# A hybrid attention layer whose engines follow a written-out list: one weight sum by an accumulating transfer, a second buffer for branch A's logarithms, other lead times

## The chip, the core and the metric

The kernel runs on one core of a Trainium2 chip. The core has a TensorE (PE, matmul, with its weight loads as PEld), a VectorE (DVE), a ScalarE (ACT), a GpSimd (POOL) and a SyncE (SP, which here only issues transfers). Each engine works off its own queue in order and waits on semaphores for the others. The metric is the device time of one execution in microseconds; the time of a kernel is the median of its runs.

## The reference, cut to what matters

One layer: a normed input, one input projection to eight parts, two kinds of attention with eight heads each, a SiLU gate, one output projection and the residual. Everything is fp32.

```python
h = rms_norm(x, norm_g)                         # (512, 2048)
qa, ka, va, ga, qb, kb, vb, gb = split(h @ w_in)   # w_in (2048, 8192), 8 parts of 1024
# branch A, stick-breaking, 8 heads of 128, strictly causal
z = qa @ ka.T * 128 ** -0.5
log_stay = where(s < t, log_sigmoid(-z), 0)
after = reverse_cumsum(log_stay) - log_stay
ya = where(s < t, exp(log_sigmoid(z) + after), 0) @ va
# branch B, 8 heads: RMS-normed q and k, learned bias by distance, softmax over the band
yb = softmax(qb_n @ kb_n.T * 128 ** -0.5 + bias) @ vb
x = x + concat(ya * silu(ga), yb * silu(gb)) @ w_out   # w_out (2048, 2048)
```

## The kernel before

**The projections.** The input projection is cut into 32 units of 256 columns (`NU`; eight head pairs `NG`, for each q, k, v and gate; even pairs belong to branch A, odd ones to B). Every product is fp32 by two fp32r parts: a high half (a cast on ScalarE) and a low half (operand minus high half, on VectorE), and matmuls of high with high, high with low, and low with high. Units are multiplied by Winograd's form of Strassen's scheme: seven products in place of eight, for which blocks of weights, blocks of activations and products are added and subtracted. Three units at the start and one at the end work in small steps; the 28 between (`MAJOR`) work with whole blocks.

**A major unit.** Its weights come as four blocks of 128 x 1024, A11, A21, A22 and A12 (`block_load`). `block_sums` forms from them on VectorE (L506) s1 = A21 + A22, s3 = A21 - A11 (in A21's place), s2 = A11 - s1 (in A11's place), and s4 = s2 + A12 (again in A11's place, after s2 has been split). `block_split` splits each of the seven operands, in the order A11, s3, s2, A22, s1, A12, s4: the high half on ScalarE (L543), the low half on VectorE (L544). There are three buffers for the split halves, so a split may begin when the operand three stages earlier has been multiplied. A stage is one operand against its activations on PE: eight matmuls of 128x512 (L803, the weights' high half against both halves of the activations) and eight of 128x256 (L805, their low half against the activations' high half). `chain` collects the products: three PSUM banks, in which several stages accumulate; after stages 0, 1 and 2 a copy of the bank to SBUF on ScalarE (L565, L568, L571), which must be done before stages 2, 3 and 4 add into that bank; later VectorE adds a bank to such a copy (L573); at the end a copy (L584) and a closing add on VectorE (L588) into the unit's result buffer, which also sets free the buffer of the copies for the next unit's L565. The result buffer must have been emptied by the attention of the head pair before.

**Attention.** `score_a` (branch A) works on a block of 128 rows: mask (L1292), absolute value (L1293), exponential (L1294), logarithm (L1295) in the buffer `L`, then relu (L1296) and a scan from the right (L1297) in the buffer `W`, a difference (L1300) and an exponential (L1302). There is one `L`, held from before the block's scores until its scan, and three `W`. `score_b` (branch B) uses a `bias` buffer, loaded once per head by `load_bias` from SP, with a memset of one corner on GpSimd (L1393). `turn` transposes the weights on PE (L1424) and splits them (L1432, L1433); `values` multiplies with v and then with the gate (L1490) and stores to DRAM; `gates` scales and applies the SiLU (L1505, L1506, with two table loads on ScalarE).

**What sets the order.** Nothing is left to the engines. While the program is being built, a small planner plays the kernel through with a clock of its own (`schedule`): every piece of work is a generator that yields conditions and operations (`Op`) with an engine, an assumed cost and a due time. Whenever an engine is free, the ready operation with the earliest due time is issued next, and that becomes the engine's instruction order. Due times are either relative to when PE will need the result (`need(k, before)`: the assumed time until product k begins, less `before`) or absolute. Without one, an operation is due `LATE` after it is announced; that holds for nearly all of attention and the SiLU. An engine that is free takes what is ready, even if its due time is far off; nothing is interrupted. On PE, attention goes ahead of projection products. Waits between engines are semaphores that follow from the data; a wrong guess of the planner costs time.

```python
self.due = due if callable(due) else (lambda d=clock[0] + LATE if due is None else due: d)
k = min(ready[e], key=lambda k: (k[0].due(), k[3]))
```

Of the kernel before, what the change touches and what calls it, by code (L numbers as in the profile page):

```python
# [72 lines left out]
def trunk_kernel(ctx: ExitStack, tc: tile.TileContext, xT, xn, wi, wqk, wo, ng, qg, kg, rel, out):  # L73
# [100 lines left out]

            self.hold = False

    LATE = 1.5

    RATE, LANDING = 290e3, 2.4

# [42 lines left out]
    def schedule(next_product):  # L223

        while True:
            while True:

                go_on = False
                for w in sorted(waiting, key=lambda w: w[0]):
                    if w in waiting and w[1]():  # L230
                        waiting.remove(w)
                        advance(w[2], w[0])
                        go_on = True
                if not go_on:
# [24 lines left out]
            while events and events[0][0] <= clock[0] + 1e-9:  # L259
                heapq.heappop(events)[2]()  # L260
# [93 lines left out]
    before_major = [n for n in olds if n < step_of[MAJOR[0], 0]]  # L354

    blocks = [1 if steps_[n][0] >= NU or len(x) > 3 and not major(steps_[n][0]) else 2 for n, x, a in program]
    takes = [(0.71 if wide(x) else 0.354 if major(steps_[n][0]) else 0.37) * b_ for (n, x, a), b_ in zip(program, blocks)]
    begins = [0.0]
    for t_ in takes:
        begins.append(begins[-1] + t_)  # L360
# [121 lines left out]
    def own(m, name):  # L482
# [4 lines left out]
        if all((m, x) in raw_ for x in RAW):  # L487
            done.add(("taken", m))

    def block_load(m, name):  # L490
        yield from own(m, name)
        k = at_step[stage(m, 5 if name == "A12" else 0 if name == "A11" else 1)]
        w = wi[chunk(MAJOR[m])]
        h, c = 2 * (name[2] == "2"), P * (name[1] == "2")

        def fn():
            for i in range(2):
                sp.dma_start(raw_[m, name][:, i * 4 * P:(i + 1) * 4 * P].rearrange("p (a b) -> p a b", b=P), w[h + i, :, :, c:c + P])

        yield Op("SP", 0.94, fn, need(k, 10), lag=P * 4096)  # L500
        done.add(("src", m, name))

    def block_sums(m):
        yield from own(m, "s1")
        r = lambda x: raw_[m, x]
        tt = lambda o, a, b, op: DV(1024, lambda: dve.tensor_tensor(out=r(o), in0=r(a), in1=r(b), op=op), need(at_step[stage(m, 1)], 6))  # L506
        k = [at_step[stage(m, p)] for p in range(NP)]
        has = lambda *x: lambda: all(("src", m, y) in done for y in x)
        yield has("A21", "A22")
        op = tt("s1", "A21", "A22", ALU.add)  # L510
        op.due = need(k[1], 5)
        yield op
        done.add(("src", m, "s1"))
        yield has("A11")
        op = tt("A21", "A21", "A11", ALU.subtract)
        op.due = need(k[1], 4)
        yield op
        done.add(("src", m, "s3"))
        yield lambda: ("w", stage(m, 0)) in done
        op = tt("A11", "A11", "s1", ALU.subtract)  # L520
        op.due = need(k[2], 4)
        yield op
        done.add(("src", m, "s2"))
        yield has("A12")
        yield lambda: ("w", stage(m, 2)) in done
        op = tt("A11", "A11", "A12", ALU.add)
        op.due = need(k[6], 4)
        yield op
        done.add(("src", m, "s4"))
        yield lambda: ("w", stage(m, 5)) in done  # L530
        unclaim(("raw", m, "A12"))

    def block_split(m, p):
        name, n, c = ORDER[p][0], stage(m, p), NP * m + p
        k = at_step[n]
        yield lambda: ("hl", c - 1) in done if c else all(("hi", x, q) in done for q in range(2) for x in having[q] if x <= before_major[-1])
        yield lambda: ("src", m, name) in done and avail(HL[c % 3])
        t = raw_[m, {"s3": "A21", "s2": "A11", "s4": "A11"}.get(name, name)]
        v = claim(("hl", c), HL[c % 3]).rearrange("p (a b) -> p a b", a=2)
        at_end.setdefault(last_of[n], []).append(("hl", c))  # L540
        mats[n] = v.rearrange("p a (b c) -> p a b c", c=P)
        done.add(("hl", c))
        yield AC(1024, lambda: act.copy(v[:, 0, :], t), need(k, 3.0))  # L543
        yield DV(1024, lambda: dve.tensor_tensor(out=v[:, 1, :], in0=t, in1=v[:, 0, :].bitcast(F32), op=ALU.subtract), need(k, 1.0))  # L544
# [7 lines left out]
    def chain(m):  # L552
# [12 lines left out]
        yield AC(512, lambda: act.copy(c[:, 0, :], b[0]), need(k[2], 1.5))  # L565
        done.add(("before", m, 2))
        yield there(1)
        yield AC(512, lambda: act.copy(c[:, 3, :], b[1]), need(k[3], 1.5))  # L568
        done.add(("before", m, 3))
        yield there(2)  # L570
        yield AC(512, lambda: act.copy(c[:, 2, :], b[0]), need(k[4], 1.5))  # L571
        done.add(("before", m, 4))
        add = lambda i, x: lambda: dve.tensor_tensor(out=c[:, i, :], in0=x, in1=c[:, i, :], op=ALU.add)  # L573
        yield there(3)
        yield DV(512, add(2, b[1]), clock[0] + 3)
        free(1)
        yield there(4)
        yield DV(512, add(3, b[0]), need(k[6], 1.5))
        done.add(("before", m, 6))
        yield there(5)  # L580
        yield DV(512, add(0, b[2]), clock[0] + 3)
# [618 lines left out]
    C = {}  # L1200
    qk, vv, wt, wT, tm, bias = {}, {}, {}, {}, {}, {}
    owner = {}
    live = dict(L=[], W=[])

    def take(who):

# [7 lines left out]

    def buffer(tag, n=1):

        ring, most = live[tag], dict(L=1, W=3)[tag]
        yield lambda: not any(ring[i] for i in range(len(ring) + n - most) if i >= 0)
        ring += [True] * n
        return [len(ring) - n + i for i in range(n)]  # L1220

    def drop(tag, i):
        live[tag][i] = False
# [36 lines left out]
    def score(g, h):  # L1260

        n = head(g, h)
        yield lambda: all(("prep", n, k) in done for k in range(2)) and (n == 0 or ("scores", n - 1) in done)
        for b in range(NT):
            i = None
            if g % 2 == 0:
                i, = yield from buffer("L")
            else:
                yield lambda: n in bias
            k, = yield from buffer("W")  # L1270
            z_ = yield from take(("score", n, b))
# [16 lines left out]
    def score_a(n, b, z_, z, L, W, w, i, k):  # L1288
# [96 lines left out]
    def load_bias(g, h):  # L1385
        n = head(g, h)

        before = n - 1 if h else n - 3
        yield lambda: ("unit", 4 * g) in done and (before < 0 or ("soft", before) in done)
        b = tmp([P, S], "bias", "bias")  # L1390
        row = rel[g // 2 * 2 + h]
        yield L_(P * 2048, lambda: sp.dma_start(b, bass.AP(tensor=row.tensor, offset=row.offset, ap=[[1, P], [1, S]])))
        yield G(0.4, lambda: pool.memset(b[0:CHUNK, 0:CHUNK], NEG_BIG))  # L1393
        bias[n] = b

    def score_b(n, b, z_, z, p_, w, k):
        st = tmp([P, 2], "st", "st", bufs=4)
# [208 lines left out]
```

## Time and profile before

| | |
|---|---|
| runs | 918.74, 919.42, 920.57 us; median 919.42 |
| profiled execution | 919.27 us, span 917.5 us, granted clock 0.998 |
| busy | PE 903.3, weight loads 802.3, VectorE 824.1, ScalarE 635.5, GpSimd 17.8 us |
| weight sums on VectorE (L506) | 112 of 128x1024, 136.3 us, 1217 ns each |
| splits (L543 on ScalarE, L544 on VectorE) | 196 each, 206.3 and 237.8 us |
| weight loads from `wi` on SP | 254 of 256 KB, 3.5 us median to landing |
| accumulating transfers on GpSimd (L1090) | 12 of 256 KB, from HBM into SBUF, in the last 130 us |

The page gives each engine's busy share of the span, the span in 40 slices, the transfer queues, the chain of work that ended last, the costliest groups of instructions with the idle time of their engine in front of them and what ended it, and the transfers. A busy PE is not PE at its peak, since matmuls are pipelined and their ends modelled. The groups' names are source lines; "L803 <-ACT arena L565 2.8" is 2.8 us in which PE stood ahead of a matmul of line 803 until ScalarE's instruction of line 565 had ended.

### The profile page before, as it was taken

What the parts mean: (1) busy time and instruction counts of PE and PEld (TensorE: products, weight loads), DVE (VectorE), ACT (ScalarE), POOL (GpSimd) and SP (SyncE); (2) the same over time, 40 slices, a digit from 0 to 9 for tenths busy, and PEclk for the clock granted to TensorE, in tenths of its full rate; (3) what the DMA queues carried; (4) which work ended last, traced back from release to release, by engine and by line L of the source; (5) the groups of instructions that cost most, each with busy time, mean ns of one, the idle gap of its engine ahead of it and who ended that gap; (6) DMA issues with size and microseconds to landing.
All of it is one profiled execution on the core that took longest, in us unless ns stands there. A gap on an engine that the chain in (4) does not pass through costs nothing.

```text
span 917.5 us, 15033 instructions
## 1 busy us (share of the span) xinstructions
PE 903.3 (98%) x5504; PEld 802.3 (87%) x5504; DVE 824.1 (90%) x1307; ACT 635.5 (69%) x1202; POOL 17.8 (2%) x35
## 2 busy tenths in 40 slices
PE   9999999999999999999999999999999999999997
PEld 6898888878888888888888888888888988899997
DVE  8989899979998998998989989999998998978785
ACT  8775777697687668875877688658778885634342
POOL 0000000000000000000000000000000000101011
PEclk9999999999999999999999999999999999999999
DMA  9663343323332433333333333333332536656371
GB/s 321 210 204 93 83 124 93 104 80 91 109 101 73 135 104 92 102 105 104 93 92 115 107 92 101 117 106 96 94 102 76 150 115 217 170 188 171 129 184 47
DMA packets 149914, 112.14 MB, mean 122 GB/s; under 512 B 7248, under 2 KB 126544, under 8 KB 149840
## 3 DMA queue, kind: packets, MB, share of 16 engines
q1 hardware_dynamic: 147696, 107.51, 38.2%
q0 software_dynamic: 1728, 3.15, 2.1%
q8 instruction: 43, 0.70, 0.3%
q10 hardware_dynamic: 416, 0.52, 0.2%
q14 instruction: 31, 0.25, 0.1%
HBM read 102.77 MB, written 8.39 MB: 121 GB/s over the span
## 4 chain that ended last, share of the span: by engine, by line
PE 83%; DVE 7%; ACT 6%; issue 2%; DMA 1%; SPq 0%; DVEq 0%; ACTq 0%
PE banks L803 36%; PE banks L805 18%; PE banks L732 16%; PE banks L730 8%; PE banks L1424 2%; PE banks L793 1%; DMA arena<-in_wi 1%; DVE parts L449 1%; DVE parts L544 1%; PE banks L1326 1%; ACT parts L543 1%; PE banks L1447 1%; DVE arena L506 1%; PE banks L794 1%; DVE xt L675 1%
## 5 line engine op out<-in xcount | busy, mean ns | idle before, releaser
L803 PE MATMUL banks<-x,parts 128*128 128x512 f32 x1568 | 503.1, 402 | 5.5 <-ACT arena L565 2.8
L805 PEld LDWEIGHTS banks<-x,parts 128*128 128x128 f32 x1568 | 294.3, 188 | 72.9 <-DVE parts L544 3.8
L805 PE MATMUL banks<-x,parts 128*128 128x256 f32 x1568 | 311.2, 280 | 0.5 <-DVE parts L544 0.4
L543 ACT CAST parts<-arena 128x1024 fp32r<-128x1024 f32 x196 | 206.3, 1057 | 100.6 <-PE banks L803 59.4
L544 DVE TENSOR_TENSOR parts<-arena,parts 128x1024 fp32r<-128x1024 f32 x196 | 237.8, 1219 | 17.4 <-ACT parts L543 17.0
L803 PEld LDWEIGHTS banks<-x,parts 128*128 128x128 f32 x1568 | 241.4, 190 | 7.9 <-ACT arena L565 3.4
L506 DVE TENSOR_TENSOR arena<-arena 128x1024 f32<-128x1024 f32 x112 | 136.3, 1217 | 3.9 <-DMA arena<-in_wi 3.8
L732 PE MATMUL banks<-parts,x 128*128 128x256 f32 (+1 forms) x672 | 134.6, 298 | 0.0
L445 ACT CAST parts<-arena 128x1024 fp32r<-128x1024 f32 (+3 forms) x84 | 77.2, 926 | 76.6 <-PE banks L732 39.5
L732 PEld LDWEIGHTS banks<-parts,x 128*128 128x128 f32 x672 | 107.4, 191 | 4.1 <-DVE parts L449 0.4
L449 DVE TENSOR_TENSOR parts<-arena,parts 128x1024 fp32r<-128x1024 f32 (+3 forms) x84 | 89.3, 1070 | 20.9 <-ACT parts L445 20.5
L730 PE MATMUL banks<-parts,x 128*128 128x256 f32 (+1 forms) x336 | 100.2, 298 | 0.0
L732 PE MATMUL banks<-x,parts 128*128 128x256 f32 (+1 forms) x320 | 75.4, 327 | 0.5 <-DVE parts L449 0.3
L730 PEld LDWEIGHTS banks<-parts,x 128*128 128x128 f32 x336 | 63.9, 190 | 3.3
L573 DVE TENSOR_TENSOR arena<-banks,arena 128x512 f32<-128x512 f32 x84 | 57.3, 683 | 9.0 <-PE banks L805 8.9
L732 PEld LDWEIGHTS banks<-x,parts 128*128 128x128 f32 x320 | 53.8, 190 | 7.0 <-DVE parts L449 2.0
L730 PE MATMUL banks<-x,parts 128*128 128x256 f32 (+1 forms) x160 | 52.9, 331 | 0.0
L1432 ACT CAST wth<-banks 128x128 fp32r<-128x128 f32 (+1 forms) x64 | 27.5, 430 | 10.9 <-PE banks L1424 10.8
L1433 DVE TENSOR_TENSOR wtl<-banks,wth 128x128 fp32r<-128x128 f32 (+1 forms) x64 | 31.0, 485 | 4.1 <-ACT wth L1432 4.1
L588 DVE TENSOR_TENSOR c<-arena 128x1024 f32<-128x1024 f32 x28 | 34.1, 1218 | 0.0
L730 PEld LDWEIGHTS banks<-x,parts 128*128 128x128 f32 x160 | 30.5, 191 | 3.3 <-ACT parts L445 0.5
L1424 PE MATMUL banks<-ident,W 128*128 128x128 f32 x160 | 28.4, 276 | 1.1 <-DVE wtl L1433 0.7
(206 smaller groups left out, 1085.3 us busy)
## 6 DMA issues: line engine op xcount, KB each, us to landing
arena<-in_wi SPq DMA_DIRECT2D x254, 256.0 KB, 3.5
arena<-in_wo SPq DMA_DIRECT2D x64, 256.0 KB, 3.9
xs<-in_xn SPq DMA_DIRECT2D x16, 256.0 KB, 4.3
mixd<-c SPq DMA_DIRECT2D x16, 256.0 KB, 2.3
out<-co SPq DMA_DIRECT2D x16, 256.0 KB, 5.1
x<-mixd SPq DMA_DIRECT2D x12, 256.0 KB, 3.9
co<-in_xn POOLq DMA_DIRECT2D x12, 256.0 KB, 6.4
x<-in_xT SPq DMA_DIRECT2D x8, 256.0 KB, 5.4
```

Source lines behind the costliest of these rows:

```text
L445: act.copy(whl[n, part][:, 0, c], t)
L449: yield DV(c.stop - c.start, lambda: dve.tensor_tensor(out=l[:, c], in0=t, in1=h[:, c].bitcast(F32), op=ALU.subtract), need(k, 0.5))
L506: tt = lambda o, a, b, op: DV(1024, lambda: dve.tensor_tensor(out=r(o), in0=r(a), in1=r(b), op=op), need(at_step[stage(m, 1)], 6))
L543: yield AC(1024, lambda: act.copy(v[:, 0, :], t), need(k, 3.0))
L544: yield DV(1024, lambda: dve.tensor_tensor(out=v[:, 1, :], in0=t, in1=v[:, 0, :].bitcast(F32), op=ALU.subtract), need(k, 1.0))
L573: add = lambda i, x: lambda: dve.tensor_tensor(out=c[:, i, :], in0=x, in1=c[:, i, :], op=ALU.add)
L588: yield DV(1024, lambda: dve.tensor_tensor(out=t_, in0=c[:, :, :H], in1=c[:, :, H:], op=ALU.add), clock[0] + 1.5)
L730: pe.matmul(o, lh, rh, start=start, stop=False, **kw)
L732: pe.matmul(o, x, y, start=False, stop=stop and (x is ll) != early, **kw)
L803: pe.matmul(both, mats[n][:, 0, j, :], X[j][:, :, i, :], start=p in (0, 1, 5) and j == 0, stop=False, skip_group_check=True)
L805: pe.matmul(o[:, :H], mats[n][:, 1, j, :], X[j][:, 0, i, :], start=False, stop=j == NJ - 1, skip_group_check=True)
L1424: pe.transpose(t[:, j * P:(j + 1) * P], src[:, j * P:(j + 1) * P], ident)
```

## The change

Four things are changed.

- s4 is no longer a VectorE instruction. An accumulating transfer, issued by GpSimd, adds A12 to the buffer that holds s2, both in SBUF (28 transfers, 512 KB each). The planner assumes 1.1 us for its issue and 7 us until it has landed, and its due time is 14 us ahead of stage 6.
- Branch A's logarithms may use the `bias` buffer when `L` is taken, except for the last block of a pair's second head (`either`). The bias load of the first head of a pair of branch B waits for that last block to begin, and the load is kept in a ring of one (`live["bias"]`).
- Lead times: `LATE` is 4.5 in place of 1.5; the sums s1 and s3 are due 4.5 and 3.5 us ahead in place of 5 and 4 (s2 stays at 4), a split's high half 2.5 in place of 3.0, its low half 1.5 in place of 1.0, the three bank copies 1.0 in place of 1.5, the add ahead of stage 6 2.0 in place of 1.5.
- The planner's assumed time of a major product is 0.351 in place of 0.354 us in `takes`; a membership test in its loop is dropped. Two expressions of `block_load` become functions (`piece`, `source`).

```diff
-    LATE = 1.5
+    LATE = 4.5
+
+    AHEAD = 4.5, 3.5, 4, 2.5, 1.5, 1.0, 2.0
...
-                    if w in waiting and w[1]():
+                    if w[1]():
...
-    takes = [(0.71 if wide(x) else 0.354 if major(steps_[n][0]) else 0.37) * b_ for (n, x, a), b_ in zip(program, blocks)]
+    takes = [(0.71 if wide(x) else 0.351 if major(steps_[n][0]) else 0.37) * b_ for (n, x, a), b_ in zip(program, blocks)]
...
-        op.due = need(k[1], 5)
+        op.due = need(k[1], AHEAD[0])
...
-        op.due = need(k[1], 4)
+        op.due = need(k[1], AHEAD[1])
...
-        op.due = need(k[2], 4)
+        op.due = need(k[2], AHEAD[2])
         yield op
         done.add(("src", m, "s2"))
         yield has("A12")
         yield lambda: ("w", stage(m, 2)) in done
-        op = tt("A11", "A11", "A12", ALU.add)
-        op.due = need(k[6], 4)
-        yield op
+        yield G(1.1, lambda: pool.dma_start(r("A11"), r("A12"), accum_op=ALU.add), need(k[6], 14))
+        there = clock[0] + 7.0
+        later(there, lambda: None)
+        yield lambda: clock[0] >= there - 1e-9
         done.add(("src", m, "s4"))
...
-        yield AC(1024, lambda: act.copy(v[:, 0, :], t), need(k, 3.0))
-        yield DV(1024, lambda: dve.tensor_tensor(out=v[:, 1, :], in0=t, in1=v[:, 0, :].bitcast(F32), op=ALU.subtract), need(k, 1.0))
+        yield AC(1024, lambda: act.copy(v[:, 0, :], t), need(k, AHEAD[3]))
+        yield DV(1024, lambda: dve.tensor_tensor(out=v[:, 1, :], in0=t, in1=v[:, 0, :].bitcast(F32), op=ALU.subtract), need(k, AHEAD[4]))
...
-        yield AC(512, lambda: act.copy(c[:, 0, :], b[0]), need(k[2], 1.5))
+        yield AC(512, lambda: act.copy(c[:, 0, :], b[0]), need(k[2], AHEAD[5]))
...
-        yield DV(512, add(3, b[0]), need(k[6], 1.5))
+        yield DV(512, add(3, b[0]), need(k[6], AHEAD[6]))
...
-    live = dict(L=[], W=[])
+    live = dict(L=[], W=[], bias=[])
...
+    def either(other):
+
+        yield lambda: not any(live["L"]) or other and not any(live["bias"])
+        tag = "bias" if any(live["L"]) else "L"
+        live[tag].append(True)
+        return tag, len(live[tag]) - 1
...
             if g % 2 == 0:
-                i, = yield from buffer("L")
+                last = h and b == NT - 1
+                if last:
+                    done.add(("last", n))
+                i = yield from either(not last)
...
-            L = tmp([P, S], "L", "L")[:, :w] if g % 2 == 0 else None
+            L = tmp([P, S], i[0], "L")[:, :w] if g % 2 == 0 else None
...
-        drop("L", i)
+        drop(*i)
...
-        before = n - 1 if h else n - 3
-        yield lambda: ("unit", 4 * g) in done and (before < 0 or ("soft", before) in done)
+        yield lambda: ("unit", 4 * g) in done and (("soft" if h else "last", n - 1) in done)
+        k, = yield from buffer("bias")
         b = tmp([P, S], "bias", "bias")
...
         bias[n] = b
+        yield lambda: ("soft", n) in done
+        drop("bias", k)
```

More of the change, by code (lines that the diff above doesn't have):

```diff
@@ L488, in own, with piece, source @@
             done.add(("taken", m))
+    def piece(m, name, i):
+        return raw_[m, name][:, i * 4 * P:(i + 1) * 4 * P].rearrange("p (a b) -> p a b", b=P)
+    def source(m, name, i):
+        h, c = 2 * (name[2] == "2"), P * (name[1] == "2")
+        return wi[chunk(MAJOR[m])][h + i, :, :, c:c + P]
     def block_load(m, name):
@@ L492, in block_load @@
         k = at_step[stage(m, 5 if name == "A12" else 0 if name == "A11" else 1)]
-        w = wi[chunk(MAJOR[m])]
-        h, c = 2 * (name[2] == "2"), P * (name[1] == "2")
         def fn():
             for i in range(2):
-                sp.dma_start(raw_[m, name][:, i * 4 * P:(i + 1) * 4 * P].rearrange("p (a b) -> p a b", b=P), w[h + i, :, :, c:c + P])
+                sp.dma_start(piece(m, name, i), source(m, name, i))
         yield Op("SP", 0.94, fn, need(k, 10), lag=P * 4096)
@@ L564, in chain @@
         c = claim(("cmb", m), CMB).rearrange("p (a b) -> p a b", a=4)
-        yield AC(512, lambda: act.copy(c[:, 0, :], b[0]), need(k[2], 1.5))
+        yield AC(512, lambda: act.copy(c[:, 0, :], b[0]), need(k[2], AHEAD[5]))
         done.add(("before", m, 2))
         yield there(1)
-        yield AC(512, lambda: act.copy(c[:, 3, :], b[1]), need(k[3], 1.5))
+        yield AC(512, lambda: act.copy(c[:, 3, :], b[1]), need(k[3], AHEAD[5]))
         done.add(("before", m, 3))
         yield there(2)
-        yield AC(512, lambda: act.copy(c[:, 2, :], b[0]), need(k[4], 1.5))
+        yield AC(512, lambda: act.copy(c[:, 2, :], b[0]), need(k[4], AHEAD[5]))
         done.add(("before", m, 4))
@@ L1215, in buffer @@
     def buffer(tag, n=1):
-        ring, most = live[tag], dict(L=1, W=3)[tag]
+        ring, most = live[tag], dict(L=1, W=3, bias=1)[tag]
         yield lambda: not any(ring[i] for i in range(len(ring) + n - most) if i >= 0)
```

## Prediction

> **What bounds the kernel now.** First the page's engine totals, then PE and the other engines in five stretches cut where the work changes: start, first heads, steady units, hand-over to the output projection, output projection. (Columns: stretch, length, busy us and count per engine, granted clock, DMA share, GB/s.)
>
> ```profile
> PE 903.3 (98%) x5504; PEld 802.3 (87%) x5504; DVE 824.1 (90%) x1307; ACT 635.5 (69%) x1202; POOL 17.8 (2%) x35
> ...
> 0.00:70.00 70.00, 68.08 (x356) 57.70 (x357) 62.07 (x107) 53.45 (x100) 2.21 (x10) 1.00 0.75 241
> 70.00:207.00 137.00, 131.46 (x766) 114.97 (x765) 124.27 (x196) 102.24 (x203) 0.29 (x2) 0.99 0.33 97
> 207.00:690.00 483.00, 482.52 (x2857) 424.66 (x2856) 446.55 (x662) 355.61 (x692) 0.73 (x5) 1.00 0.35 101
> 690.00:760.00 70.00, 68.68 (x431) 60.45 (x430) 63.03 (x137) 59.45 (x129) 0.94 (x2) 1.00 0.38 123
> 760.00:917.50 157.50, 152.59 (x1100) 144.53 (x1099) 128.15 (x209) 64.74 (x80) 13.61 (x16) 1.00 0.53 155
> ```
>
> PE is the bound, and its 5504 matmuls are not touched. It is idle 14.17 us in all: 1.92, 5.54, 0.48, 1.32 and 4.91 us by stretch. The first is the start and the last the tail behind the last matmul, where this change has nothing; so there are 7.3 us of plain idle time to win, three quarters of it in the 137 us from 70 to 207. The 483 us after that are already full. Next, whom PE waits for, from the groups by line:
>
> ```profile
> L803 PE MATMUL banks<-x,parts 128*128 128x512 f32 x1568 | 503.1, 402 | 5.5 <-ACT arena L565 2.8 <-ACT arena L568 2.1 <-ACT arena L571 0.6
> L805 PEld LDWEIGHTS banks<-x,parts 128*128 128x128 f32 x1568 | 294.3, 188 | 72.9 <-DVE parts L544 3.8
> L543 ACT CAST parts<-arena 128x1024 fp32r<-128x1024 f32 x196 | 206.3, 1057 | 100.6 <-PE banks L803 59.4 <-issue 13.7 <-DVE arena L506 13.6
> L544 DVE TENSOR_TENSOR parts<-arena,parts 128x1024 fp32r<-128x1024 f32 x196 | 237.8, 1219 | 17.4 <-ACT parts L543 17.0
> L506 DVE TENSOR_TENSOR arena<-arena 128x1024 f32<-128x1024 f32 x112 | 136.3, 1217 | 3.9 <-DMA arena<-in_wi 3.8
> ```
>
> So the stops are not for DVE's weight sums. They are for ScalarE's copies of a finished stage's bank (L565, L568, L571: 5.5 us), and in small pieces for the low half of a split (L544: 3.8 us, seen by the weight loads). The largest of them, in order of time (start, length, instruction, idle before it):
>
> ```profile
> 192.99 1.28 ACT L1505 ACT_TABLE_LOAD   x1
> 194.29 1.06 ACT L1505 ACTIVATE c<-c 128x1024 f32<-128x1024 f32 x1
> 195.37 1.28 ACT L1506 ACT_TABLE_LOAD   x1
> 196.66 0.60 ACT L1407 ACTIVATE W<-W,st,yn 128x256 f32<-128x256 f32 x1
> ...
> 198.41 0.73 ACT L1407 ACTIVATE W<-W,st,yn 128x384 f32<-128x384 f32 x1
> 199.02 0.22 ACT L1407 ACTIVATION_READ_ACCUMULATOR W<-W,st,yn 128x1 f32 x1
> 199.11 0.60 ACT L568 COPY arena<-banks 128x512 f32<-128x512 f32 x1
> 199.76 0.73 PE L803 MATMUL banks<-x,parts 128*128 128x512 f32 x2 [2.06 <-ACT arena L568]
> ```
>
> ScalarE stood 3.7 us in the SiLU and its two table loads, and then ran 2.45 us of attention (196.66 to 199.11) before the copy that PE was waiting for.
>
> **The change part by part.**
>
> *Lead times.* Work without a due time of its own (all of attention, and the SiLU) becomes due 4.5 us after it is announced, not 1.5. The splits' high half moves from 3.0 to 2.5 us ahead of its stage, the low half from 1.0 to 1.5, the bank copies from 1.5 to 1.0. Copies and high halves keep their order among themselves; both pass attention more easily, by 2.5 us of due time. I go through PE's stops one by one.
>
> (a) Stop at 199.76. The copy would follow the table load at 196.65 and be done by 197.25, before PE ran dry at 197.7: 2.06 us. The clock falls behind it as well:
>
> ```profile
> 200.00:204.00 4.00, 4.00 (x16) 3.44 (x16) 2.75 (x5) 4.00 (x8) 0.00 (x0) 0.57 0.25 66
> ```
>
> A granted clock of 0.57 over 4 us is 4 x 0.43 = 1.7 us. Together 3.8 us. (The Trainium skill, "TensorE: Matmul & The Clock Gate", section "HAM oscillation — how this bites in real kernels", asks for idle gaps of over about 3.4 us before the clock is gated. By it this stop of 2.06 us would not be the cause, the term would be 2.1 and the time 1.7 us higher. The trace has the drop right behind the stop, and I go by the trace.)
>
> (b) and (c) Two smaller stops:
>
> ```profile
> 118.55 1.29 DVE L1245 TENSOR_TENSOR qk<-c,qk 128x512 fp32r<-128x512 f32 x2
> 119.75 1.23 DVE L544 TENSOR_TENSOR parts<-arena,parts 128x1024 fp32r<-128x1024 f32 x1
> 120.89 1.23 DVE L588 TENSOR_TENSOR c<-arena 128x1024 f32<-128x1024 f32 x1
> ...
> 121.84 1.05 ACT L543 CAST parts<-arena 128x1024 fp32r<-128x1024 f32 x1
> 122.77 0.60 ACT L565 COPY arena<-banks 128x512 f32<-128x512 f32 x1
> 123.43 0.73 PE L803 MATMUL banks<-x,parts 128*128 128x512 f32 x2 [1.43 <-ACT arena L565]
> ...
> 105.40 0.58 ACT L1293 ACTIVATE L<-banks,rstds 128x384 f32<-128x384 f32 x1
> 105.88 0.36 ACT L1432 CAST wth<-banks 128x256 fp32r<-128x256 f32 x1
> 106.13 0.60 ACT L571 COPY arena<-banks 128x512 f32<-128x512 f32 x1
> 106.78 0.72 PE L803 MATMUL banks<-x,parts 128*128 128x512 f32 x2 [0.59 <-ACT arena L571]
> ```
>
> At 123.43 the copy L565 waited for the buffer that the closing add L588 frees. That add keeps its due time and passes the two L1245 (1.29 us); but a split stands between it and the copy as before, so I take 0.9 of the 1.43 us. At 106.78 L1293 and L1432 stood ahead (0.94 us): all 0.6 us go. The remaining L565 share, 2.8 - 1.43 = 1.4 us, is a stop at 78.9 behind the closing adds of the last plain unit, whose dues stay: 0.
>
> (d) The low halves: 3.8 us of waits at most. They are due 0.5 us earlier and DVE is lighter (below); I take half, 1.9.
>
> (e) A new order has stops of its own. Over the 27 units from 70 to 690 PE idles (5.54 + 0.48) / 27 = 0.22 us per unit; I charge a third of that to each of 28: 2.1 us against, bounds 0 and 28 x 0.22 = 6.2.
>
> *The fourth sum.* 28 of the 112 sums (L506) leave DVE: 28 x 1.217 = 34.1 us of its 824. Since PE waits for DVE for 3.8 us in all, they are worth no more than what (d) has. In exchange GpSimd issues 28 accumulating transfers of 512 KB. The trace has no such transfer inside SBUF; the nearest is the residual's, 256 KB from HBM:
>
> ```profile
> L1090 POOL DMA_DIRECT2D co<-in_xn x12: 862/920/1235, 789.0 to 877.3; - x12
> DMA to landing us min/median/max: 3.5/6.4/8.6
> ```
>
> With twice the bytes the landing lies between 3.5 us and 2 x 8.6 = 17.2 us; I take 8, the median and a quarter, near the list's own 1.1 + 7.0. There is a window for it. In one of the shorter units, the low half of stage 2's split (after which A11 may be overwritten), the old sum, the split of the sum, its low half and stage 6 itself stand at
>
> ```profile
> 493.29 1.20 DVE L544 TENSOR_TENSOR parts<-arena,parts 128x1024 fp32r<-128x1024 f32 x1
> ...
> 498.06 1.22 DVE L506 TENSOR_TENSOR arena<-arena 128x1024 f32<-128x1024 f32 x1
> ...
> 501.59 1.06 ACT L543 CAST parts<-arena 128x1024 fp32r<-128x1024 f32 x1
> ...
> 505.26 1.22 DVE L544 TENSOR_TENSOR parts<-arena,parts 128x1024 fp32r<-128x1024 f32 x1
> 507.19 0.72 PE L803 MATMUL banks<-x,parts 128*128 128x512 f32 x2
> ```
>
> The sum must be there 1.06 + 1.22 us before 507.19, at 504.9: 10.4 us after 494.49. Eight fit, so the term is 0; the cover is stages 2 to 5 on PE. If it is late, the split L543 stands waiting on ScalarE with bank copies and attention queued behind it, and PE waits for those. On POOL's queue only the eight bias memsets stand in its way, each waiting for its bias load. The transfers add 28 x 0.5 = 15 MB to stretches with a DMA share of 0.33 to 0.35; weight loads are issued up to 10 us ahead: 0.
>
> *Logarithms in two buffers.* The next block's absolute value no longer waits for the scan before it. The bias buffer lends itself, so the bias load comes later, after the last block of the heads before, and waits on SP with weight loads behind it (10 us ahead). Branch A's end is not what PE waits for, with one exception:
>
> ```profile
> 168.03 0.69 DVE L1490 TENSOR_TENSOR c<-banks,c 128x512 f32<-128x512 f32 x1
> ...
> 169.90 1.22 DVE L588 TENSOR_TENSOR c<-arena 128x1024 f32<-128x1024 f32 x1
> ...
> 171.16 0.59 ACT L565 COPY arena<-banks 128x512 f32<-128x512 f32 x1
> ```
>
> The first pair's product with its gate (L1490) frees the buffer that L588 writes, and the next unit's copy follows at once. Two buffers bring this forward, later dues push it back; I take 0, bounds -1.4 us and the rival below. The planner's stage price of 0.351 for 0.354 and the dropped membership test move due times by under 0.1 us in 10: 0.
>
> **Sum.** 3.8 + 0.9 + 0.6 + 1.9 - 2.1 = 5.1 us off the profiled execution's 919.27 us (span 917.5 us and 1.8 around it): 914.2. The median of the runs is 919.42, 0.15 above that execution: 914.3 us.
>
> **The rivals.**
>
> *The stops stay.* Where a split became ready just before a copy (123.43), priority does not matter, because the engine was free; the list's clock may differ from the chip's at the SiLU too. Against it: at 199 and 106 only default work stood ahead. Then (c) and half of (d) remain, 1.5 us, with 0.5 us of new stops: 918.4, no change.
>
> *Attention becomes the bound (slower).* From L1490 at 168.03 to the copy's end at 171.75 there is no slack. Behind the pair's last scan come five steps on ScalarE and VectorE (L1300, the exponential L1302, the transposed weights' high half L1432 and low half L1433, L1490 itself). If each now loses to one split (1.06 or 1.22, mean 1.14 us), L1490 comes 5.7 us later; L588, the copy and PE stop as long, and a stop over 2.06 us brings the clock's 1.7 us. From L1490 at 168.0 on, each us costs one. For it: ScalarE is 75% and DVE 91% busy there. Against it: two buffers and 1.2 us less DVE work per unit. 914.3 + 7.4 = 921.7 us.
>
> *The transfer is late (slower).* It decides from 10.4 us. At 12 us a unit like the one shown loses 1.6 us; were a fifth of the 28 so short, 9 us: 923.3. For it: 8.6 us already at half the bytes. Against it: those rows come several at once and from HBM, these singly and inside SBUF.
>
> *The change does not do what it says.* If due times hardly decide who is next, the list is nearly the same with 28 sums gone: that is the first rival's time.
>
> **How the numbers follow.** Forecast 0.62, stops stay 0.16, attention 0.13, late transfer 0.06, the rest 0.03. The forecast's own range is 909 to 917.5: down to (a) to (d) with the stop at 123 and (d) whole and no new one (919.4 - 3.8 - 1.4 - 0.6 - 3.8 = 909.8, less 0.5 for the steady stretch's idle), up to new stops at 5.3. The bounds let the time fall by 5.5 + 1.7 + 0.5 + 1.3 + 3.8 = 12.8 at the very most, 906.6. For 8 in 10 I give 907.5 to 922, which takes in the unchanged case and the attention rival. A measurement of this kernel can tell about 0.2%, 1.8 us, from no change. Faster by more than that: 0.62 and a quarter of the first rival, 0.66; within it 0.14; slower 0.20.
>
> **What would show it.** L506 x84 and 28 transfers on POOL landing in under 10 us; PE's idle time from 70 to 207 at 2 us or less and the clock there at 1.00; L803's wait on L568 and L571 gone, that on L565 near 1.4; L805's wait on L544 halved; 207 to 690 under 2.5 us idle. Wrong if L803 waits for a split behind a late sum, if L588 follows a late L1490 near 168 us, or if the steady stretch shows new stops over 6 us.

## The result, and the profile after

The changed kernel takes 913.00 us (median of four runs, 912.89 to 913.28) against 919.17 us for the kernel before beside it: ratio 0.9931, 95% interval 0.9914 to 0.9948, 6.2 us faster. The forecast was 914.3. The profiled execution has a span of 910.8 us, 6.7 less than before.

The page's engine totals, then PE and the others in the same stretches (columns as in the prediction):

```profile
PE 899.3 (99%) x5504; PEld 801.8 (88%) x5504; DVE 793.7 (87%) x1279; ACT 634.2 (70%) x1199; POOL 42.2 (5%) x63
...
0.00:70.00 70.00, 67.97 (x356) 57.61 (x357) 62.01 (x107) 53.41 (x100) 2.37 (x10) 1.00 0.75 241
70.00:207.00 137.00, 133.46 (x786) 116.75 (x786) 120.80 (x186) 100.23 (x196) 5.51 (x7) 1.00 0.46 118
207.00:690.00 483.00, 482.02 (x2861) 425.64 (x2860) 424.57 (x653) 360.20 (x711) 19.08 (x27) 1.00 0.50 125
690.00:760.00 70.00, 70.00 (x438) 62.85 (x437) 63.48 (x137) 58.80 (x117) 1.77 (x3) 1.00 0.49 155
760.00:910.80 150.80, 145.88 (x1071) 138.96 (x1069) 122.79 (x201) 61.52 (x75) 13.45 (x16) 1.00 0.52 151
```

PE's idle time by stretch is now 2.03, 3.54, 0.98, 0 and 4.92 us, 2.7 less in all: 2.0 less with the first heads, 1.3 less at the hand-over, 0.5 more in the steady units. The other 4 us are in PE's busy time for the same 5504 matmuls (903.3 to 899.3): 1.7 of them were the spell at half clock behind the stop at 199.8, which is gone (the first heads' granted clock is 1.00, not 0.99); for the other 2.3 no row names a cause. That they are waits which a matmul's modelled end hides is a guess. From the groups by line:

```profile
L811 PE MATMUL banks<-x,parts 128*128 128x512 f32 x1568 | 502.3, 402 | 3.4 <-ACT arena L573 2.4
L813 PEld LDWEIGHTS banks<-x,parts 128*128 128x128 f32 x1568 | 294.3, 188 | 71.5 <-DVE parts L552 2.0
L513 DVE TENSOR_TENSOR arena<-arena 128x1024 f32<-128x1024 f32 x84 | 102.2, 1216 | 6.1 <-DMA arena<-in_wi 5.9
L533 POOL DMA_DIRECT2D arena<-arena x28 | 24.4, 873 | 563.3 <-DMA arena<-in_wi 219.3
```

Lines have moved: matmuls L803 and L805 are L811 and L813, splits L543 and L544 are L551 and L552, the copies after stages 0, 1 and 2 (first, second and third copy below) L565, L568, L571 are L573, L576, L579, the closing add L588 is L596, the gate product L1490 is L1510. PE's waits for copies fell from 5.5 to 3.4 us, for low halves from 3.8 to 2.0.

ScalarE around the SiLU that made the largest stop before (start, length, instruction):

```profile
193.46 0.58 ACT L576 COPY arena<-banks 128x512 f32<-128x512 f32 x1
194.06 1.28 ACT L1525 ACT_TABLE_LOAD   x1
195.35 1.06 ACT L1525 ACTIVATE c<-c 128x1024 f32<-128x1024 f32 x1
196.43 1.28 ACT L1526 ACT_TABLE_LOAD   x1
197.72 0.59 ACT L579 COPY arena<-banks 128x512 f32<-128x512 f32 x1
198.21 0.49 ACT L1427 ACTIVATE W<-W,st,yn 128x128 f32<-128x128 f32 x1
```

The second copy now stands ahead of the SiLU, the third directly behind its table load, and attention after that. Before, 2.45 us of attention stood in between.

The transfer, from the view of its line:

```profile
L533 POOL DMA_DIRECT2D arena<-arena x28: 859/868/1021, 76.9 to 693.0; - x28
DMA to landing us min/median/max: 4.6/5.6/6.4
```

By these views most of the signs that the prediction named are there: 84 sums, 28 transfers landing in under 10 us, the clock at 1.00 from 70 to 207, the waits for low halves about halved, 0.98 us of idle time in the steady units. Three are not: PE is idle for 3.54 us from 70 to 207, not 2 or less; it still waits 1.0 us for second and third copies (0.8 for L576, 0.2 for L579); and it waits 2.4 us for first copies, not 1.4. The experiments show that the forecast's terms were not the whole of it.

### The profile page after: what moved, and what is told of

It is laid out like the page before. It is cut to its first block, busy times and chain, and to the rows that moved or that the text cites. A ratio compares the mean times of both kernels' runs of the same rounds, so it can differ in the third digit from the quotient of the medians.

```text
span 910.8 us, 15157 instructions
## 1 busy us (share of the span) xinstructions
PE 899.3 (99%) x5504; PEld 801.8 (88%) x5504; DVE 793.7 (87%) x1279; ACT 634.2 (70%) x1199; POOL 42.2 (5%) x63
## 3 DMA queue, kind: packets, MB, share of 16 engines
q0 software_dynamic: 5760, 17.83, 12.4%
## 4 chain that ended last, share of the span: by engine, by line
PE 82%; DVE 9%; ACT 4%; DMA 3%; issue 2%; SPq 0%; DVEq 0%; ACTq 0%
PE banks L811 34%; PE banks L813 17%; PE banks L740 17%; PE banks L738 8%; DVE parts L552 2%; DMA arena<-in_wi 2%; PE banks L1444 2%; PE banks L801 1%; DVE arena L513 1%; PE banks L1344 1%; DVE parts L451 1%; ACT parts L551 1%; PE banks L802 1%; PE banks L1467 1%; DVE xt L683 1%
## 5 line engine op out<-in xcount | busy, mean ns | idle before, releaser
L811 PE MATMUL banks<-x,parts 128*128 128x512 f32 x1568 | 502.3, 402 | 3.4 <-ACT arena L573 2.4
L813 PEld LDWEIGHTS banks<-x,parts 128*128 128x128 f32 x1568 | 294.3, 188 | 71.5 <-DVE parts L552 2.0
L813 PE MATMUL banks<-x,parts 128*128 128x256 f32 x1568 | 310.0, 279 | 1.1 <-DVE parts L552 1.1
L551 ACT CAST parts<-arena 128x1024 fp32r<-128x1024 f32 x196 | 205.7, 1053 | 114.1 <-PE banks L811 49.9
L552 DVE TENSOR_TENSOR parts<-arena,parts 128x1024 fp32r<-128x1024 f32 x196 | 237.9, 1217 | 41.4 <-ACT parts L551 40.6
L811 PEld LDWEIGHTS banks<-x,parts 128*128 128x128 f32 x1568 | 240.6, 189 | 5.7 <-ACT arena L573 3.1
L513 DVE TENSOR_TENSOR arena<-arena 128x1024 f32<-128x1024 f32 x84 | 102.2, 1216 | 6.1 <-DMA arena<-in_wi 5.9
L581 DVE TENSOR_TENSOR arena<-banks,arena 128x512 f32<-128x512 f32 x84 | 57.1, 680 | 7.0 <-PE banks L813 5.5
L533 POOL DMA_DIRECT2D arena<-arena x28 | 24.4, 873 | 563.3 <-DMA arena<-in_wi 219.3
L596 DVE TENSOR_TENSOR c<-arena 128x1024 f32<-128x1024 f32 x28 | 34.0, 1214 | 0.0
```

What stands on the lines that cost most here:

```text
L551: yield AC(1024, lambda: act.copy(v[:, 0, :], t), need(k, AHEAD[3]))
L596: yield DV(1024, lambda: dve.tensor_tensor(out=t_, in0=c[:, :, :H], in1=c[:, :, H:], op=ALU.add), clock[0] + 1.5)
L811: pe.matmul(both, mats[n][:, 0, j, :], X[j][:, :, i, :], start=p in (0, 1, 5) and j == 0, stop=False, skip_group_check=True)
L813: pe.matmul(o[:, :H], mats[n][:, 1, j, :], X[j][:, 0, i, :], start=False, stop=j == NJ - 1, skip_group_check=True)
```

## The experiments

Theory 1 was the prediction's: the later due time carries the gain, the sum off VectorE is worth the low halves' waits at most, the second log buffer nothing. Theory 2: the 34 us less on VectorE carry it. Theory 3: every new order has stops of its own, and no part carries anything.

**Each part undone.**

```diff
# no_late: the changed kernel with
-    LATE = 4.5
+    LATE = 1.5
# no_sum: the changed kernel with
-        yield G(1.1, lambda: pool.dma_start(r("A11"), r("A12"), accum_op=ALU.add), need(k[6], 14))
-        there = clock[0] + 7.0
...
+        op = tt("A11", "A11", "A12", ALU.add)
+        op.due = need(k[6], 4)
+        yield op
# no_ahead: the changed kernel with
-    AHEAD = 4.5, 3.5, 4, 2.5, 1.5, 1.0, 2.0
+    AHEAD = 5, 4, 4, 3.0, 1.0, 1.5, 1.5
# no_logs: the changed kernel with buffer("L") for either(...), and load_bias as before
-                i = yield from either(not last)
+                i, = yield from buffer("L")
```

> The changed kernel with the default due time back at 1.5 us, all else as changed. Theory 1 (the default due time carries the gain, because attention no longer stands ahead of bank copies on ScalarE): 917 to 919 us, bank-copy waits of PE back at 4 us or more, among them one of about 2 us during a SiLU with a clock drop behind it. Theory 2 (the 34 us taken off VectorE carry it): 913 to 914.5 us. Theory 3 (every new order has its own stops by chance, no part carries the gain): anywhere from 912 to 918.

> The changed kernel with the fourth sum back on VectorE (due 4 us ahead of stage 6, as before). Theory 1: 913 to 915 us, at most the 1.8 us by which the waits on low halves fell come back. Theory 2: 917 to 919 us, PE waiting for low halves again for 3.8 us. Theory 3: 912 to 918.

> The changed kernel with the lead times of sums, splits and bank copies as before (5, 4, 4, 3.0, 1.0, 1.5, 1.5), default due time 4.5. Theory 1: 913 to 914.5 us, since copies and high halves keep their order among themselves and only the low halves lose 0.5 us. Theory 2: 913 to 914.5 too. Theory 3: 912 to 918.

> The changed kernel with one buffer for branch A's logarithms and the bias load's old condition. Theory 1: 913 to 914 us in the steady stretch; but the later due times then fall on a chain with one buffer, so if the first pair's gate product (at 168 us in the kernel before) comes later, PE loses as much there, up to 4 us: 913 to 917. Theory 2: 913. Theory 3: 912 to 918.

Measured against 919.27 us for the kernel before beside them: no_late 931.51 us (ratio 1.0131, 1.0108 to 1.0154), no_sum 918.56 (0.9993, 0.9984 to 1.0003), no_ahead 919.75 (1.0006, 0.9997 to 1.0016), no_logs 937.87 (1.0203, 1.0188 to 1.0218). Without any one of these four the gain is gone, and without either of two of them (the due time, the buffers) the kernel is far slower than before. All three theories fall: 18.5 us for the due time is more than it could have gained, the buffer priced at nothing is worth 24.9, and no range for luck reached that far.

**Each part alone.**

```diff
# late_only: the kernel before with
-    LATE = 1.5
+    LATE = 4.5
# sum_only: the kernel before with the accumulating transfer in place of
-        op = tt("A11", "A11", "A12", ALU.add)
# logs_only: the kernel before with either(...) and the new load_bias in place of
-                i, = yield from buffer("L")
# takes_only: the kernel before with
-0.354 if major
+0.351 if major
```

> The kernel before with the default due time at 4.5 us in place of 1.5, nothing else. Theory 1: 915 to 916 us, the stops at 106 and 199 us and the clock drop gone, no or smaller stop at 123. Theory 2: 919. Theory 3: 914 to 921. The rival of the prediction (attention becomes the bound): 920 to 922, with L588 behind a late L1490 near 168 us.

> The kernel before with the fourth sum as an accumulating transfer, nothing else. Theory 1: 917.5 to 919 us, the stops on bank copies stay and only waits on low halves fall by 1 to 2 us. Theory 2: 914 to 915. Theory 3: 914 to 921.

> The kernel before with branch A's logarithms in two buffers and the later bias load, nothing else. Theory 1 and 2: 918.5 to 919.5 us. Theory 3: 914 to 921.

> The kernel before with the planner's price of a major product at 0.351 in place of 0.354, nothing else: a change of due times by under 0.1 us in 10, made to see how much a new order alone moves the time. Theory 1 and 2: 918.5 to 919.5 us. Theory 3: it moves by 1 us or more to either side, with stops in other places.

Measured against 919.44 us beside them: late_only 938.94 us (1.0210, 1.0194 to 1.0225), sum_only 939.17 (1.0209, 1.0194 to 1.0225), logs_only 927.88 (1.0080, 1.0060 to 1.0099), takes_only 921.17 (1.0011, 1.0002 to 1.0021). None of the four helps alone, and all ranges of theories 1 and 2 were missed; theory 3's held for takes_only alone. The last run says what a new order by itself does: ScalarE's list is the same for its first half and then differs, and the time moves by 1.7 us. So 2 us could be luck. One such run sets no limit to what luck can do; that 8 to 25 us are more than luck rests on the pairs and the steps of the due time below.

Where the time goes differs with the part. With the later due time and one log buffer, much of it is the chain at which the prediction saw its slower rival. late_only, the first pair's gate product, the closing add, the first copy, and PE:

```profile
180.46 0.69 DVE L1490 TENSOR_TENSOR c<-banks,c 128x512 f32<-128x512 f32 x1 [3.23 <-PE banks L732]
...
181.33 1.22 DVE L588 TENSOR_TENSOR c<-arena 128x1024 f32<-128x1024 f32 x1
...
182.58 0.59 ACT L565 COPY arena<-banks 128x512 f32<-128x512 f32 x1 [0.68 <-DVE c L588]
...
183.22 1.22 PE L803 MATMUL banks<-x,parts 128*128 128x512 f32 x2 [2.80 <-ACT arena L565]
```

The gate product comes 12.4 us later than before (168.03), after VectorE has stood idle for 3.23 us, the copy stands behind the closing add, and PE stops; it had already stopped 2.8 us at 174 for the pair's transposed weights. The pair's last scan shows where the delay comes from. In the kernel before, late_only, no_logs and the changed kernel:

```profile
156.63 1.22 DVE L1297 TENSOR_TENSOR_SCAN W<-L,W 128x512 f32<-128x512 f32 x1
...
165.88 1.22 DVE L1297 TENSOR_TENSOR_SCAN W<-L,W 128x512 f32<-128x512 f32 x1
...
169.16 1.22 DVE L1305 TENSOR_TENSOR_SCAN W<-L,W 128x512 f32<-128x512 f32 x1
...
152.29 1.23 DVE L1315 TENSOR_TENSOR_SCAN W<-L,W 128x512 f32<-128x512 f32 x1 [0.36 <-ACT W L1314]
```

With one buffer, 9.3 (late_only) and 12.5 us (no_logs) of delay are there before the last scan starts, in the blocks that take the buffer one after the other. With two, in the changed kernel, the scan starts 4.3 us earlier than before and the steps behind it take 4.3 us longer, so the gate product stays at 168.

The longest stop of late_only is another one, 4.14 us, behind a closing add that stood behind two L1245 (1.28 us) on a busy VectorE, the stop (b) of the prediction grown:

```profile
125.21 1.21 DVE L588 TENSOR_TENSOR c<-arena 128x1024 f32<-128x1024 f32 x1
...
127.09 1.22 PE L803 MATMUL banks<-x,parts 128*128 128x512 f32 x2 [4.14 <-ACT arena L565]
```

The clock adds to it: granted 0.95 from 70 to 207, against 0.99 before, is 6.9 us lost in that stretch against 1.7. Attention's last pair is late as well: the hand-over has 2.9, 1.5 and 1.2 us of stops for it. no_logs shows both again (gate product at 177.8 us, 2.9, 1.5 and 1.2 us at the hand-over).

With the old due time and new buffers or a lighter VectorE, ScalarE fills with attention in front of the second and third copies. no_late, ScalarE and PE at the last SiLU but one:

```profile
713.89 1.28 ACT L1525 ACT_TABLE_LOAD   x1
715.18 1.06 ACT L1525 ACTIVATE c<-c 128x1024 f32<-128x1024 f32 x1
716.26 1.28 ACT L1526 ACT_TABLE_LOAD   x1
717.55 0.21 ACT L1142 ACTIVATE rq<-nwt 128x4 f32<-128x4 f32 x1
...
718.94 0.71 ACT L1391 ACTIVATE qk<-c,qgs 128x512 fp32r<-128x512 f32 x1
719.55 0.57 ACT L576 COPY arena<-banks 128x512 f32<-128x512 f32 x1
...
720.17 0.73 PE L811 MATMUL banks<-x,parts 128*128 128x512 f32 x2 [3.09 <-ACT arena L576]
```

That is the stop of term (a) again, 3.1 us long: SiLU, then 2 us of attention, then the copy. sum_only has it twice at 4.3 us, at 392 and 580 us, in the same way. no_late also has 4.2 us of PE's waits for VectorE's add of a bank to a copy (L581), of which the kernel before and the changed one have none.

So a second theory, theory A below (theory B is chance): default due time and log buffers pull on two ends. Early dues put attention in front of the copies, and a second buffer makes more attention ready to stand there. Late dues make attention late, and the second buffer pays that back. They are right only together.

**The two together, and neither.**

```diff
# late_logs: the kernel before with
-    LATE = 1.5
+    LATE = 4.5
-                i, = yield from buffer("L")
+                i = yield from either(not last)
# no_late_no_logs: the changed kernel with the reverse
```

> The kernel before with both the default due time of 4.5 us and the two buffers for branch A's logarithms, sums on VectorE and lead times as before. Theory A (the two belong together: the later due time alone makes attention late, the second buffer alone sets more attention ahead of the bank copies): 917 to 924 us, far under the 938.9 and 927.9 of each alone; the first pair's last gate product back near 168 us, PE waiting under 1.5 us for the copies after stages 1 and 2. Theory B (a new order moves the time by chance): no relation to the two, anything from 915 to 940. If the gains of single parts simply added: 919 + 20 + 8 = 947.

> The changed kernel with default due time 1.5 us and one buffer for the logarithms: left are the accumulating transfer and the lead times. Theory A: no late attention (first pair's last gate product at 168 to 172 us, hand-over as before), but attention ahead of the copies: PE waits 3 to 12 us for the copies after stages 1 and 2, 922 to 936 us. Theory B: anything from 915 to 940. If undoing added: 913 + 18 + 25 = 956.

Measured against 919.11 us beside them: late_logs 919.98 us (1.0008, 0.9999 to 1.0018), no_late_no_logs 942.62 (1.0255, 1.0240 to 1.0270). The medians in two squares:

| | due 1.5, one buffer | due 4.5, one buffer | due 1.5, two buffers | due 4.5, two buffers |
|---|---|---|---|---|
| sum on VectorE, old lead times | 919.3 (before) | 938.9 | 927.9 | 920.0 |
| accumulating transfer, new lead times and stage price | 942.6 | 937.9 | 931.5 | 913.0 (changed) |

Added up, the single losses would have given late_logs 947 us; together they cancel to 920. Theory A holds there. In the second row no_late_no_logs came out 6.6 us above its range, with 13.1 us of waits for the second copy, and its hand-over was not as before (4.4 us idle, granted clock 0.95): the transfer, the new lead times and the stage price, without the pair, belong with the early-due failure. They pay only on top of the pair, 920.0 to 913.0. late_logs loses most of that at the hand-over, 2.84 us of idle time and 3.5 by the clock:

```profile
690.00:760.00 70.00, 67.16 (x410) 59.20 (x410) 57.38 (x127) 56.49 (x122) 0.88 (x2) 0.95 0.39 129
```

One half of theory A is seen in the first row only. There the second buffer alone raises the waits for the second and third copies (2.7 to 7.0 us, next table) and the time. In the second row it lowers both (13.1 to 9.2 us, 942.6 to 931.5), and the later due time alone gains too (937.9). The other half holds in both rows: with late dues the second buffer brings the gate product forward, from 180.5 to 167.2 and from 177.8 to 168.0.

**The due time moved either way.**

```diff
# late_3 and late_6: the changed kernel with
-    LATE = 4.5
+    LATE = 3.0     # late_3; 6.0 in late_6
```

> The changed kernel with a default due time of 3.0 us in place of 4.5. Theory A: the first pair's last gate product earlier than 168 us (155 to 166), PE's waits for the copies after stages 1 and 2 between the 1.0 us at 4.5 and the 9.2 us at 1.5: 914 to 924 us. Theory B: no trend, 912 to 930.

> The changed kernel with a default due time of 6.0 us in place of 4.5. Theory A: the copies after stages 1 and 2 cost PE 1 us at most, but the first pair's last gate product comes at 169 to 175 us and L588 with its stop behind it, and the hand-over to the output projection has stops again: 914 to 924 us. Theory B: no trend, 912 to 930.

Measured against the same 919.11 us: late_3 916.19 us (0.9973, 0.9963 to 0.9983), late_6 935.61 (1.0180, 1.0165 to 1.0195). Side by side, PE's waits for the second and third copies (from the waits of PE) and the start of the first pair's last gate product (from the timeline):

| kernel | default due | log buffers | second and third copy, us | gate product, us | time, us |
|---|---|---|---|---|---|
| before | 1.5 | 1 | 2.7 | 168.0 | 919.3 |
| sum_only | 1.5 | 1 | 12.3 | 171.6 | 939.2 |
| takes_only | 1.5 | 1 | 2.7 | 168.5 | 921.2 |
| logs_only | 1.5 | 2 | 7.0 | 146.7 | 927.9 |
| no_late | 1.5 | 2 | 9.2 | 151.4 | 931.5 |
| no_late_no_logs | 1.5 | 1 | 13.1 | 168.9 | 942.6 |
| late_3 | 3.0 | 2 | 3.2 | 157.0 | 916.2 |
| changed | 4.5 | 2 | 1.0 | 168.0 | 913.0 |
| late_logs | 4.5 | 2 | 1.0 | 167.2 | 920.0 |
| no_ahead | 4.5 | 2 | 1.2 | 165.7 | 919.8 |
| no_sum | 4.5 | 2 | none | 173.9 | 918.6 |
| late_only | 4.5 | 1 | none | 180.5 | 938.9 |
| no_logs | 4.5 | 1 | none | 177.8 | 937.9 |
| late_6 | 6.0 | 2 | 0.7 | 174.3 | 935.6 |

Along the due time both columns go the way theory A says: every kernel due at 1.5 waits 2.7 to 13.1 us for these copies, every one due at 4.5 or later at most 1.2; and the gate product moves later with the due time (151, 157, 168, 174 for two buffers and the transfer). The columns do not give the time: no_sum and late_6 are nearly alike in both and 17 us apart. late_6 has the late gate product and the stops at the hand-over that were expected, but is 12 us over its range. Its waits show, beside the chain at the gate product, 3.1 us for VectorE's adds of a bank (L581; 3.4 in no_late_no_logs), which theory A does not explain, and stops for splits of the mixed activations at the end (late_logs and no_ahead have fewer):

```profile
PE banks L740 <- DVE xbbias L726: 1.2, 1, 1.2
PE banks L740 <- DVE xbwth L726: 1.0, 1, 1.0
PE banks L738 <- ACT xbbias L725: 1.0, 1, 1.0
PE banks L740 <- DVE x L726: 0.9, 1, 0.9
```

In the program these splits wait until the last pair's attention has released the buffers in which they are made, so attention that is late at the end holds them up.

**What the transfer is worth where the pair is in place.** no_sum against the changed kernel: the steady units are as good (483 us with 0.06 us idle), the hand-over too (0.01 idle); all of the 5.6 us are lost with the first heads:

```profile
70.00:207.00 137.00, 128.85 (x751) 112.43 (x750) 122.12 (x196) 98.08 (x197) 0.29 (x2) 0.99 0.32 93
207.00:690.00 483.00, 482.94 (x2866) 426.48 (x2865) 446.07 (x664) 360.06 (x700) 0.72 (x5) 1.00 0.35 101
690.00:760.00 70.00, 69.99 (x447) 63.26 (x446) 65.44 (x137) 60.00 (x127) 0.88 (x2) 1.00 0.43 139
```

```profile
173.93 0.69 DVE L1509 TENSOR_TENSOR c<-banks,c 128x512 f32<-128x512 f32 x1 [0.68 <-PE banks L739]
...
174.60 1.22 DVE L595 TENSOR_TENSOR c<-arena 128x1024 f32<-128x1024 f32 x1
...
176.50 0.88 PE L810 MATMUL banks<-x,parts 128*128 128x512 f32 x2 [2.61 <-ACT arena L572]
```

The gate product at 173.9, 6 us later than with the transfer, then the closing add, the first copy and PE: 2.6 us, after 2.3 us at 169 for the same pair's weights, and a spell at half clock behind them (0.99 over the stretch). That is the chain of late_only in small. VectorE is 89% busy there; the sums taken off it bring the first pair's attention back to 168. In the kernel before, PE's direct waits for VectorE, where the prediction looked, do not show this.

The new lead times alone on the kernel before were not run, and the stage price was not undone in the changed kernel. no_ahead loses 6.8 us against the changed kernel, from the steady units on, with more waits for low halves (changed: 2.0 us); which of the seven numbers does it is open.

```profile
L813 PEld LDWEIGHTS banks<-x,parts 128*128 128x128 f32 x1568 | 294.3, 188 | 73.0 <-DVE parts L552 4.3
```

## Why the prediction was right, and where it was not

The time, the sign and the range held: 5.1 us forecast, 6.2 measured. Term by term:

- (a) The stop at 199.8 and its half clock are gone (3.8 forecast, 3.8 found), though not quite as described: the second copy, for which PE stopped, now passes the SiLU as well, and it is the third that directly follows the table load. With the stop the half clock went; here the row was a better guide than the 3.4 us of the Trainium skill, "TensorE: Matmul & The Clock Gate", section "HAM oscillation — how this bites in real kernels".
- (b) The stop at 123 is 0.39 us in place of 1.43, 1.0 gained for 0.9 forecast; (c) is gone, 0.6; the stop at 78.9 stays, 1.39 us, as forecast.
- (d) The weight loads' waits on low halves fell by 1.8 us; forecast 1.9. Weight loads overlap matmuls (801.8 and 899.3 us busy in a span of 910.8), and the matmuls' own waits on them rose from 0.4 to 1.1 us, so it is not shown that the 1.8 us became time.
- (e) New stops were put at 2.1 us. Beside the low halves, which (d) counts, PE has a new one of 0.67 us behind a first copy and 0.8 and 0.2 for second and third copies: 1.7.
- Not in the sum, so put at 0: the hand-over, from 1.32 us of idle to none.

That is 3.8 + 1.0 + 0.6 + 1.8 - 1.7 = 5.5 us, and 6.8 with the hand-over, against 6.7 between the spans. With (d) open and 2.3 us of PE's busy time without a cause, so close a fit is in part luck.

*The fourth sum* landed in 5.6 us, at most 6.4, where 8 were taken and 10.4 allowed: PE and the splits do not wait for it (ScalarE once, 0.4 us), and the late-transfer rival is out.

The step that failed is the attribution. "I take 0, bounds -1.4 us" for the logarithms, and "worth no more than what (d) has" for the sum, were both wrong: in place they are worth 24.9 and 5.6 us. The new due time was priced only by what it removes, and the buffer and the sum only against the kernel before. The 0 stood for two moves of the gate product, earlier by the buffer and later by the due time, and neither was sized; that they came out even, 168.03 before and 167.96 after, is luck. The edge itself was in the prediction: no slack between the first pair's gate product and the stop behind it, each us costing one. From the changed kernel to late_only the gate product moves by 12.5 us and the copy L573 (there L565) by 12.8. An earlier product does not bring that copy forward: no_late has the product 16.6 us earlier and the copy at 169.74. The changed kernel still stands on that edge:

```profile
167.96 0.69 DVE L1510 TENSOR_TENSOR c<-banks,c 128x512 f32<-128x512 f32 x1 [0.92 <-PE banks L740]
168.57 1.21 DVE L596 TENSOR_TENSOR c<-arena 128x1024 f32<-128x1024 f32 x1
...
169.81 0.58 ACT L573 COPY arena<-banks 128x512 f32<-128x512 f32 x1 [0.26 <-DVE c L596]
...
170.45 0.73 PE L811 MATMUL banks<-x,parts 128*128 128x512 f32 x2 [0.67 <-ACT arena L573]
```

The slower rival, given 0.13, saw the right place. Its size was 5.7 us of delay, from five steps behind the last scan that each lose to a split; with one buffer the delay is 10 to 12 us, most or all of it there before that scan, and the last pair's delay at the hand-over comes on top. The steps behind the scan did lengthen, by 4.3 us in the changed kernel, but there the buffer made up for it. What kept it away is what the prediction named against it, the second buffer and the lighter VectorE, without pricing either. That due times hardly decide who is next, the last rival, is out: taking the due time back costs 18.5 us.

Not settled: why the transfer alone, on the kernel before, moves two SiLUs to where they stop PE for 4.3 us; which of the parts empties the hand-over of stops (PE's idle time there is 0.01 us in no_sum, 2.84 in late_logs, which differ only in lead times and stage price, and 0.26 in no_ahead, which has the old lead times with the transfer and the new price; late_3 has 2.25); and why VectorE's adds stop PE in no_late, no_late_no_logs and late_6.

## What to carry to other kernels

A list of who waits for whom names the last link only: work with no direct wait on it can hold the chain that does, so price an edit also against slack that another edit of the same change uses up. Priorities have two sides; when one class of work is moved back, look for the point at which that class itself becomes due, and find the buffer that limits it, before counting the stops that go. When parts of a change are tried one at a time and each loses, they may still gain together, so try the pairs that pull on opposite ends.

## What was not expected of the hardware

**Accumulating transfers inside SBUF landed sooner, by the median, than the residual's from HBM with half the bytes.** 512 KB land in 4.6 to 6.4 us, median 5.6, and its issue takes GpSimd 0.87 us; the residual's 256 KB from HBM (see the prediction's row) took 3.5 to 8.6, median 6.4, with an issue of 0.92. The smallest of the residual's is the quickest of all, and they are issued in groups of four (789.0 to 795.7 us in the kernel before) while these go one per unit, so the runs do not tell whether the source or the crowd makes the difference. The row of half the size bounded it badly from above.

**The clock falls after stops of very different length.** A stop of 2.06 us was followed by a half clock in the kernel before. In late_6 one of 1.65 us that began at 211.8 was; in no_late_no_logs one of 2.28 us that began at 616.9 was not. The windows over each (late_6, then no_late_no_logs; the granted clock is the third number from the end):

```profile
211.00:218.00 7.00, 5.01 (x18) 3.90 (x18) 6.97 (x9) 1.32 (x2) 0.00 (x0) 0.76 0.25 75
```

```profile
616.00:624.00 8.00, 5.72 (x33) 4.84 (x32) 7.97 (x9) 2.58 (x3) 0.00 (x0) 1.00 0.22 66
```

Over 7 us 0.76 is 1.7 us lost, the same as in the kernel before. Length alone does not decide. (The Trainium skill, "TensorE: Matmul & The Clock Gate", section "What's actually happening", has the clock set by how busy PE was over a free-running window; that would fit stops of one length with and without a drop, but no run here separates the window's phase from the load around the stop.)
